# Out-projection of a decoder trunk: quarter sums by accumulating transfers, the residual seeded into PSUM, signs turned

## The chip, the core and the metric

The kernel runs on one core of a Trainium2 chip. TensorE (PE, with its weight loads shown as PEld) multiplies, VectorE (DVE) and ScalarE (ACT) do elementwise work, GpSimd (POOL) does a little arithmetic and issues transfers, SyncE (SP) issues most loads from HBM. Products land in PSUM, which here has eight banks of 128x512 float32; everything else on the core lives in SBUF. The metric is the time of one execution on the device in microseconds (us).

## The reference, cut to what matters

Two layers over 256 tokens of width 2048. In each layer the input is normalised and projected to q, k, v and three convolution parts; attention and a gated short convolution give two blocks of 1024 columns; one shared output projection adds them to the residual x; then comes a squared-ReLU MLP of width 8192.

```
for l in range(DEPTH):                                   # 2
    h = _rmsnorm(x, attn_norm_g[l])
    proj = h @ w_in[l]                                   # q k v gate_b gate_c conv_in
    ...
    x = x + jnp.concatenate([attn, conv], axis=-1) @ w_out[l]     # 2048 x 2048
    hm = _rmsnorm(x, mlp_norm_g[l]) @ w_up[l]
    x = x + jnp.square(jax.nn.relu(hm)) @ w_down[l]
```

All of it is float32.

## The kernel before

**Arithmetic.** Each float32 operand of a matmul is split into a rounded part `hi` (ScalarE, type float32r) and a remainder `lo` (VectorE, the value minus `hi`); a product is three matmuls, hi x hi, hi x lo, lo x hi (`TERMS`). A matmul takes a 128x128 block of activations as weights and streams 128x512 of the weight matrix.

**Seven products.** In part of the projections a block of two 128-row chunks of the contraction (a "pair", index i) times two 512-column chunks is not formed from eight products of quarters but from seven, with sums of quarters on both sides. The activation quarters are A11, A21, A12, A22 and the sums S1 to S4 (made by `BySeven.sums_of`); the weight quarters are two loads of 512 KB, `left` and `right`, and four sums `t`. The seven products gather in their own PSUM banks `prods[1..7]` over several pairs, and `results` joins them with a few adds. In the plan constants, an entry `("s", i)` is a seven-product pair and `(n, i)` an ordinary one for column chunk n.

**Stages.** Per layer: q and k side by side, v with attention behind it, the convolution parts, then the out-projection in a left half (columns 0 to 1023, interleaved with the gate's columns, plan `LEFT`) and a right half (columns 1024 to 2047, plan `RIGHT`), then the MLP. The right half's plan is

```
RIGHT = ((0, 0), (0, 1), (1, 0), (1, 1), (0, 4), (1, 4), ("s", 2), (0, 5), (1, 5), ("s", 3),
         (0, 6), (0, 7), (1, 6), (1, 7))
```

An ordinary pair is 12 matmuls and one load of 512 KB; a seven-product pair is 21 matmuls and two loads. While the right half runs, the first two chunks of the new x are already normalised and transposed for the MLP (`norm.chunk`, in the background), and the third and fourth follow as soon as the right half has finished them.

**Weights.** `Weights.take` makes the jobs of the next three entries ahead of the one that it returns. A plain job loads into one of four `raw` rooms and splits into `whi`/`wlo`, three rooms each (tags `hi`, `lo`). The jobs of a seven-product pair are `plain` (loads, the split `w7b` of B11 and B21, the split of B22 into `whi`/`wlo`), `sums` (on VectorE the four sums `w7t`, lines 916, 917, 921, 922, and the split `w7x` of the first two) and `more` (the split `w7y` of the last two). `w7b` and `w7t` lie in the pool of tag "b" with eight rooms, which also holds the four `cat` tiles (the activations of the out-projection, four 128-row chunks each) and the activation sums; `w7x` and `w7y` lie in the two "bias" rooms. In `seven` the products come in the order 1, 2, 3 (plain quarters), 5, 7 (`w7x`), 6, 4 (`w7y`).

**Order.** TensorE's order is the program's. On the other engines and the queues a planner sets the order once, when the kernel is built, from a model of the times and the program's order as priority; each engine and each queue then works in that order and waits for semaphores. Rooms of a pool are handed on by such waits.

**Ends.** In `results` the seven products become e1 to e4 (one ScalarE copy, lines 972 to 976), which `add` puts onto x (line 980) when the half is done; the two ordinary chunks are added to x by lines 1061 and 1167. The first matmul into a bank opens it (`start=True`) and so overwrites what was there. The MLP's down-projection uses the same seven products (`quarters`, lines 1330 to 1334; the activation sums in `square`, lines 1452 to 1455; `seven_onto`).

Of the kernel before, what the change touches and what calls it, by code (L numbers as in the profile page):

```python
# [15 lines left out]
P = 128  # L16
# [117 lines left out]
def trunk(ctx: ExitStack, tc: tile.TileContext, x, w_in, w_out, conv_w, q_norm_g, k_norm_g,  # L134
# [370 lines left out]

    class Norm:
# [10 lines left out]
        def chunk(self, n, wait):  # L517
# [5 lines left out]
            for j in range(2):  # L523
# [12 lines left out]
                else:  # L536
                    y = wide(f"ny{pair}").rearrange("p (k s) -> p k s", k=2)
                    for i in range(2):
# [5 lines left out]
                    self.sums_of(pair, *(y[:, i, t * P:(t + 1) * P]  # L544
                                         for i in range(2) for t in range(NT)))
# [288 lines left out]
    A11, A21, A12, A22, S1, S2, S3, S4 = range(8)  # L834

    class BySeven:
# [9 lines left out]
        def sums_of(self, i, a11, a21, a12, a22):  # L846
# [18 lines left out]
        def jobs(self, w, i, cols, in_keys=False):  # L865
# [44 lines left out]
            def sums():  # L910
                left, right = mine["raw"]
                pool, tag = (self.kpool, "kL") if in_keys else (self.pool, "b")
                t = mine["t"] = pool.tile([P, 4, CH], F32, tag=tag, name="w7t")

                with behind(in_keys or self.rooms_of == 8):
                    nc.vector.tensor_sub(t[:, 0], right[:, 0], left[:, 0])
# [5 lines left out]
                nc.vector.tensor_sub(t[:, 3], left[:, 1], t[:, 2])  # L922
                return made
# [4 lines left out]

            return [plain, sums, more]

        def form(self, i, pa, a):

            if a >= S1:
                return self.sums[i][pa][:, a - S1]
# [3 lines left out]
        def product(self, n, i, a, b, start, stop):  # L938

            for m, (pa, pw) in enumerate(TERMS):  # L940
                nc.tensor.matmul(self.prods[n], self.form(i, pa, a), b[pw],  # L941
                                 start=(start and m == 0), stop=(stop and m == 2))

        def pair(self, i, chunks, starts=(), last=False):

            for n, accs in chunks:
                hi, lo = self.weights.take()
                for j in range(2):
# [8 lines left out]
                    for t, pa, pw in steps:  # L957
# [3 lines left out]
                            stop=(last and j == 1 and (pa, pw) == TERMS[-1]))  # L961
                    work.tick()

        def results(self, n):
# [7 lines left out]
            nc.scalar.activation(e1, prods[1], AF.Copy)  # L972
            nc.vector.tensor_add(e2, prods[6], e1)
            nc.vector.tensor_add(e4, prods[5], e2)
            nc.vector.tensor_add(x22, prods[5], x22)
            nc.vector.tensor_add(e3, prods[7], e2)

            def add():
                for x_, e in ((x11, e1), (x21, e3), (x12, e4), (x22, e3)):
                    nc.vector.tensor_add(x_, x_, e)  # L980

            return add
# [15 lines left out]
        def left(self, acts, cv):  # L998
# [8 lines left out]
            def column(c):  # L1007
# [8 lines left out]
                if c % 2 and i in SEVEN_LEFT + SEVEN_RIGHT:  # L1016
                    self.sums_of(i, *(y[:, k, t * P:(t + 1) * P]
                                      for k in range(2) for t in range(NT)))

            def banks():  # L1020
# [3 lines left out]
                for n in (5, 7, 4):  # L1024
                    prods[n] = bank(f"po{l}{n}")

            for j, (what, i) in enumerate(LEFT):
# [4 lines left out]
                elif what == "a":  # L1032
# [5 lines left out]
                    self.product(2, i, A12, b21, start, not {"a", 0} & rest)  # L1038
                    self.product(3, i, S4, b22, start, not {"a", 1} & rest)
                    self.product(5, i, S1, self.t1, start, end)  # L1040
                    work.tick()
                elif what == "b":
# [5 lines left out]
                    if end:  # L1048
                        add = self.results(0)
                else:  # L1050
                    opening = what == 1 and 8 not in prods
                    if opening:
                        prods[8] = ps.tile([P, CH], F32, tag="av", name=f"po{l}8", bufs=1)
                    accs = ((prods[2], prods[4]), (prods[3], prods.get(8)))
# [698 lines left out]
```

## Time and profile before

| | |
|---|---|
| time, two runs | 2112.37 and 2113.86 us, median 2113.11 us |
| profiled execution, first to last instruction (its span) | 2110.7 us |
| median above that span | 2.4 us |
| granted TensorE clock, mean | 1.000 |
| HBM read | 440.52 MB |
| loads of w_out | 64 of 512 KB, 4.5 us from issue to landing |
| right half in layer 0 and in layer 1 | about 337 to 381 us and 1386 to 1430 us |

The profiled execution's own time is known only by its span; what lies around it is taken as the 2.4 us between span and median. A line of the profile's groups has source line, engine, operation, what it writes from what it reads, shape and count, then busy time, mean ns of one, and the idle time of the engine before it with what ended that. A line of the timeline has start and duration in us, engine, source line, operation and count. In the waits, a line gives who waited, for what, then the total in us, how often, and the longest.

### The profile page before, as it was taken

The page shows a single profiled execution, that of the slowest core. Times are in us where ns is not written, and L with a number is a line of the kernel's source. Part 1 is how long each engine was busy: PE and PEld are TensorE (multiplying, and loading weights), DVE is VectorE, ACT ScalarE, POOL GpSimd, SP SyncE. Part 2 cuts the span into 40 slices and gives each one's busy share as a digit, 9 for nine tenths or more (in the row PEclk, how much of TensorE's full clock was granted, in tenths as well). Part 3 has the DMA queues.
Part 4 walks back from the last instruction along what each step waited for, and adds up shares of the span by engine and source line. Part 5 has one row for each costly group of instructions (what it writes and reads, how often), then busy time and mean ns, then how long its engine had stood idle before and what let it go on. Part 6 is the DMA issues. An engine that isn't in the chain of part 4 may idle for free.

```text
span 2110.7 us, 29252 instructions
## 1 busy us (share of the span) xinstructions
PE 2105.2 (100%) x10809; PEld 1799.0 (85%) x10809; DVE 1834.6 (87%) x2525; ACT 1407.5 (67%) x1823; POOL 189.4 (9%) x226
## 2 busy tenths in 40 slices
PE   9999999999999999999999999999999999999999
PEld 7888888888888888888888888888888888888887
DVE  7888788898888888799888887988988888888998
ACT  6777566676776766666566775657676677675664
POOL 2211120000000000011101121000000000000110
PEclk9999999999999999999999999999999999999999
DMA  7655575887777777789566456668777777777993
GB/s 265 205 154 167 171 216 182 289 259 229 230 238 229 231 232 230 251 291 310 171 220 188 152 170 185 195 193 290 255 238 229 229 230 238 230 229 260 315 309 113
DMA packets 312607, 476.01 MB, mean 226 GB/s; under 512 B 12723, under 2 KB 209669, under 8 KB 312464
## 3 DMA queue, kind: packets, MB, share of 16 engines
q1 hardware_dynamic: 284752, 406.76, 60.7%
q0 software_dynamic: 27520, 67.24, 10.1%
q8 instruction: 85, 1.39, 0.3%
q14 instruction: 58, 0.48, 0.1%
q10 hardware_dynamic: 192, 0.15, 0.0%
HBM read 440.52 MB, written 33.58 MB: 225 GB/s over the span
## 4 chain that ended last, share of the span: by engine, by line
PE 98%; DMA 1%; POOL 1%; DVE 1%; issue 0%; ACT 0%; ACTq 0%; DVEq 0%
PE upc L1427 31%; PE pr L1470 14%; PE dn L1551 8%; PE gc L481 4%; PE ci L481 4%; PE gb L433 4%; PE v L456 3%; PE q L958 3%; PE o L958 3%; PE k L958 3%; PE dn L1470 3%; PE po L941 2%; PE dn L1645 2%; PE pr1r L1470 2%; PE pr0r L1470 2%; PE po L958 2%
## 5 line engine op out<-in xcount | busy, mean ns | idle before, releaser
L1427 PE MATMUL upc<-nT,uhi 128*128 128x512 f32 x1920 | 454.7, 389 | 0.0
L1427 PEld LDWEIGHTS upc<-nT,uhi 128*128 128x128 f32 x1920 | 360.2, 188 | 74.7
L1292 DVE TENSOR_TENSOR ulo<-uraw,uhi 128x1024 fp32r<-128x1024 f32 x256 | 312.3, 1222 | 109.8 <-ACT f L1459 91.5
L341 ACT ACTIVATE whi<-raw 128x1024 fp32r<-128x1024 f32 x232 | 244.7, 1058 | 180.2 <-issue 21.8
L1291 ACT ACTIVATE uhi<-uraw 128x1024 fp32r<-128x1024 f32 x256 | 270.6, 1057 | 135.7 <-PE upc L1427 115.4
L342 DVE TENSOR_TENSOR wlo<-raw,whi 128x1024 fp32r<-128x1024 f32 x232 | 284.3, 1234 | 53.1 <-ACT whi L341 46.9
L1427 PEld LDWEIGHTS upc<-nT,ulo 128*128 128x128 f32 x1920 | 246.2, 191 | 9.4
L1427 PE MATMUL upc<-nT,ulo 128*128 128x256 f32 x1920 | 249.1, 283 | 0.0
L1317 ACT ACTIVATE bh<-draw 128x1536 fp32r<-128x1536 f32 x86 | 128.3, 1492 | 103.7 <-PE pr L1470 82.1
L1318 DVE TENSOR_TENSOR bl<-draw,bh 128x1536 fp32r<-128x1536 f32 x86 | 151.3, 1759 | 11.4 <-ACT bh L1317 10.9
L1551 PE MATMUL dn<-whi,fb 128*128 128x512 f32 x480 | 152.0, 389 | 0.0
L1470 PE MATMUL pr<-bh,f 128*128 128x512 f32 x360 | 121.4, 391 | 0.0
L341 ACT ACTIVATE whi<-uraw 128x1024 fp32r<-128x1024 f32 x60 | 63.7, 1062 | 72.0 <-PE dn L1551 58.5
L1437 ACT ACTIVATE ev<-upc 128x512 f32<-128x512 f32 x120 | 72.0, 600 | 54.0 <-PE upc L1427 54.0
L1317 ACT ACTIVATE t24h<-t 128x1024 fp32r<-128x1024 f32 x86 | 91.4, 1063 | 23.7 <-PE pr L1470 15.9
L1551 PEld LDWEIGHTS dn<-whi,fb 128*128 128x128 f32 x480 | 90.1, 188 | 18.6
L1318 DVE TENSOR_TENSOR t24l<-t,t24h 128x1024 fp32r<-128x1024 f32 x86 | 104.9, 1220 | 0.2
L1330 DVE TENSOR_TENSOR t<-draw 128x1024 f32<-128x1024 f32 x86 | 105.0, 1221 | 0.1
L1318 DVE TENSOR_TENSOR t13l<-t,t13h 128x1024 fp32r<-128x1024 f32 x86 | 104.9, 1220 | 0.0
L1317 ACT ACTIVATE t13h<-t 128x1024 fp32r<-128x1024 f32 x86 | 91.5, 1063 | 8.1 <-DVE t L1330 2.9
L1470 PE MATMUL pr<-t13h,f 128*128 128x512 f32 x240 | 93.8, 391 | 0.0
L1551 PE MATMUL dn<-wlo,fb 128*128 128x512 f32 x240 | 93.4, 389 | 0.0
(528 smaller groups left out, 4383.9 us busy)
## 6 DMA issues: line engine op xcount, KB each, us to landing
uraw<-in_w_up_dram SPq DMA_DIRECT2D x128, 1024.0 KB, 6.3
raw<-in_w_in_dram SPq DMA_DIRECT2D x191, 512.0 KB, 4.2
draw<-in_w_down_dram SPq DMA_DIRECT2D x180, 512.0 KB, 5.3
raw<-in_w_out_dram SPq DMA_DIRECT2D x64, 512.0 KB, 4.5
uraw<-in_w_down_dram SPq DMA_DIRECT2D x60, 512.0 KB, 6.8
hid0p<-f POOLq DMA_DIRECT2D x17, 512.0 KB, 3.5
fb<-hid0p POOLq DMA_DIRECT2D x17, 512.0 KB, 8.0
hid1p<-f POOLq DMA_DIRECT2D x17, 512.0 KB, 3.5
```

Source lines behind the costliest of these rows:

```text
L341: pair = (nc.scalar.activation(hi, raw, AF.Copy), nc.vector.tensor_sub(lo, raw, hi.bitcast(F32)))
L342: nc.vector.tensor_sub(lo, raw, hi.bitcast(F32)))
L481: nc.tensor.matmul(acc[:, f, 0] if part else acc[:, f], wt[:, k % 4, fs], a.ap[:, 0, k % KG] if part else a.ap[:, :, k % KG], start=(part ...
L958: nc.tensor.matmul(accs[t], a.ap[:, pa, k % KG, t * P:(t + 1) * P], (hi, lo)[pw][:, j], start=(j == 0 and (pa, pw) == (0, 0) and (n, t) in ...
L1291: pair = (nc.scalar.activation(hi, src, AF.Copy), nc.vector.tensor_sub(lo, src, hi.bitcast(F32)))
L1292: nc.vector.tensor_sub(lo, src, hi.bitcast(F32)))
L1317: keep(nc.scalar.activation(hi, src, AF.Copy))
L1318: keep(nc.vector.tensor_sub(lo, src, hi.bitcast(F32)))
L1330: keep(nc.vector.tensor_sub(t[:, 0:2], raw[:, 0::2], raw[:, 1::-1]))
L1427: nc.tensor.matmul(acc[:, 0] if part else acc, wt[part][:, k], a.ap[:, 0, k % KG] if part else a.ap[:, :, k % KG], start=(part == 0 and kh ...
L1470: nc.tensor.matmul(prods[n], f[:, pa, a], b[pw], start=(start and m == 0), stop=(stop and m == 2))
L1551: nc.tensor.matmul(prods[p], f[:, pa, 2 * k + t], b[pw][:, n], start=(p in starts and k == 0 and m == 0), stop=(stop and k == 1 and m == 2))
```

## The change

1. **Quarter sums of the right half by transfers.** For the two seven-product pairs of the right half the jobs are new: `whole`, `summed`, `last`. Both loads go into one tile `w7r` of tag "b". After the plain quarters have been split, four transfers from POOL's queue add one quarter onto another in place (`accum_op=ALU.add`); what stands in the tile afterwards are the four sums, which are split into `w7x` and `w7y` as before. VectorE's four adds and `w7t` are gone there.
2. **Signs.** Since such a transfer can only add, the weight sums become pure additions everywhere (left half, q/k, MLP too), and the activation sums and the joining of products turn their signs to match. S3 and S1 now lie beside each other and are made by one operation where the quarters lie in one tile (`quarters_of`, `square`). In the q/k pairs all four weight sums are made ahead of the first split.
3. **Residual into the banks.** `seed` copies x into the ordinary banks by ScalarE (three banks of the left half, four of the right), and no matmul opens these. `results` then writes into x what it used to put into extra tiles, and the extra adds onto x are gone except one in the left half.

```diff
-    A11, A21, A12, A22, S1, S2, S3, S4 = range(8)
+    A11, A21, A12, A22, S3, S1, S2, S4 = range(8)
...
             v = wide(f"sv{i}").rearrange("p (s c) -> p s c", c=P)
-            nc.vector.tensor_add(v[:, 0], a21, a22)
-            nc.vector.tensor_sub(v[:, 1], v[:, 0], a11)
-            nc.vector.tensor_sub(v[:, 2], a11, a21)
-            nc.vector.tensor_sub(v[:, 3], a12, v[:, 1])
+            if both is None:
+                nc.vector.tensor_sub(v[:, 0], a11, a21)
+                nc.vector.tensor_sub(v[:, 1], a21, a22)
+            else:
+                nc.vector.tensor_sub(v[:, 0:2], *both)
+            nc.vector.tensor_sub(v[:, 2], v[:, 1], a11)
+            nc.vector.tensor_add(v[:, 3], a12, v[:, 2])
...
+                def rest():
+                    nc.vector.tensor_add(t[:, 2], t[:, 0], right[:, 1])
+                    nc.vector.tensor_add(t[:, 3], left[:, 1], t[:, 2])
+
                 with behind(in_keys or self.rooms_of == 8):
-                    nc.vector.tensor_sub(t[:, 0], right[:, 0], left[:, 0])
-                    nc.vector.tensor_sub(t[:, 1], right[:, 1], right[:, 0])
+                    nc.vector.tensor_add(t[:, 0], left[:, 0], right[:, 0])
+                    nc.vector.tensor_add(t[:, 1], right[:, 0], right[:, 1])
                 room = self.biasp.tile([P, 2, 2, CH], F32R, tag=self.spare, name="w7x")
+                if self.rooms_of == 8:
+                    rest()
                 made = two(room, t[:, 0:2])
-
-                nc.vector.tensor_add(t[:, 2], t[:, 1], left[:, 0])
-                nc.vector.tensor_sub(t[:, 3], left[:, 1], t[:, 2])
+                if self.rooms_of != 8:
+                    rest()
                 return made
...
+            def whole():
+
+                raw = mine["raw"] = self.pool.tile([P, 2, 2, CH], F32, tag="b", name="w7r")
+                for n in range(2):
+                    nc.sync.dma_start(
+                        raw[:, :, n], w[2 * P * i:2 * P * (i + 1),
+                                        cols[n]:cols[n] + CH].rearrange("(k p) c -> p k c", p=P))
+                room = self.pool.tile([P, 2, 2, CH], F32R, tag="b", name="w7b")
+                b11, b21 = two(room, raw[:, :, 0])
+                hi = wpool.tile([P, 2, CH], F32R, tag="hi", name="whi")
+                lo = wpool.tile([P, 2, CH], F32R, tag="lo", name="wlo")
+                b22 = split(hi[:, 0], lo[:, 0], raw[:, 1, 1])
+                for k, n, by in ((0, 0, (0, 1)), (0, 1, (1, 1)), (1, 1, (0, 0)), (1, 0, (1, 1))):
+                    nc.gpsimd.dma_start(raw[:, k, n], raw[:, by[0], by[1]], accum_op=ALU.add)
+                return b11, b21, b22
+
+            def summed():
+                room = self.biasp.tile([P, 2, 2, CH], F32R, tag=self.spare, name="w7x")
+                return two(room, mine["raw"][:, 0])
+
+            def last():
+                room = self.biasp.tile([P, 2, 2, CH], F32R, tag=self.spare, name="w7y")
+                return two(room, mine["raw"][:, 1])[::-1]
+
+            if by_transfer:
+                return [whole, summed, last]
             return [plain, sums, more]
...
+        def seed(self, *places):
+
+            for n, t, acc in places:
+                nc.scalar.activation(acc, xs[n][:, t], AF.Copy)
 
         def results(self, n):
...
-            room = self.tmp.tile([P, 2, CH], F32, tag="ao", name="es", bufs=1)
-            e1, e2, e3 = room[:, 0], wide("e2"), room[:, 1]
-            e4 = self.kpool.tile([P, CH], F32, tag="kL", name="es4")
-            nc.scalar.activation(e1, prods[1], AF.Copy)
-            nc.vector.tensor_add(e2, prods[6], e1)
-            nc.vector.tensor_add(e4, prods[5], e2)
-            nc.vector.tensor_add(x22, prods[5], x22)
+            e2, e3 = wide("e2"), x21 if n else wide("e3")
+            nc.scalar.activation(x11, prods[1], AF.Copy)
+            nc.vector.tensor_add(e2, prods[6], x11)
+            nc.vector.tensor_sub(x12, prods[5], e2)
             nc.vector.tensor_add(e3, prods[7], e2)
-
-            def add():
-                for x_, e in ((x11, e1), (x21, e3), (x12, e4), (x22, e3)):
-                    nc.vector.tensor_add(x_, x_, e)
-
-            return add
+            nc.vector.tensor_sub(x22, prods[5], e3)
+            if not n:
+                nc.vector.tensor_add(x21, x21, e3)
...
-                    self.weights.jobs += self.jobs(w, i, (2 * CH, 3 * CH))
+                    self.weights.jobs += self.jobs(w, i, (2 * CH, 3 * CH), by_transfer=True)
...
-            opened, add = set(), None
+            for n in range(2):
+                self.seed(*((2 + n, t, accs[n][t]) for t in range(NT)))
...
-                    keep(nc.vector.tensor_sub(t[:, 0:2], raw[:, 0::2], raw[:, 1::-1]))
+                    keep(nc.vector.tensor_add(t[:, 0:2], raw[:, 1:3],
+                                              raw[:, 0:1].to_broadcast([P, 2, CH])))
...
-                    nc.vector.tensor_add(h[:, S1], h[:, A21], h[:, A22])
+                    nc.vector.tensor_sub(h[:, S3:S1 + 1], h[:, A11:A21 + 1], h[:, A21:A22 + 1:2])
                     nc.vector.tensor_sub(h[:, S2], h[:, S1], h[:, A11])
-                    nc.vector.tensor_sub(h[:, S3], h[:, A11], h[:, A21])
-                    nc.vector.tensor_sub(h[:, S4], h[:, A12], h[:, S2])
+                    nc.vector.tensor_add(h[:, S4], h[:, A12], h[:, S2])
```

More of the change, by code (lines that the diff above doesn't have):

```diff
@@ L1048, in left @@
                     if end:
-                        add = self.results(0)
+                        self.results(0)
                 else:
@@ L1157, in right @@
                     if i == SEVEN_RIGHT[-1]:
[L1158 removed]
+                        self.results(2)
                     continue
[L1160 to L1164 removed]
+                self.pair(i, [(what, accs[what])], (), not {"s", what} & rest)
                 if not {"s", what} & rest:
```

56 lines of the change are left out of this document (26 added, 30 removed).

## The prediction

> **What bounds the kernel now.** I read the page's first part, then the waits of the weight loader, then the stage that the change touches by windows, and last its single instructions. The page:
>
> ```profile
> span 2110.7 us, 29252 instructions
> PE 2105.2 (100%) x10809; PEld 1799.0 (85%) x10809; DVE 1834.6 (87%) x2525; ACT 1407.5 (67%) x1823; POOL 189.4 (9%) x226
> ```
>
> TensorE lacks 5.5 us of the span (2110.7 - 2105.2). A busy PE can hide slow issue, so the waits of its loader come next, whole kernel, longest first, cut to those that touch the change:
>
> ```profile
> PEld po0r L941 <- DVE w7y L880: 0.5, 1, 0.5
> PEld po L941 <- DVE w7y L880: 0.2, 1, 0.2
> ```
>
> and the windows (columns: stretch, length, then busy time of PE, PEld, DVE, ACT, POOL, clock, DMA share, GB/s) of the out-projection's right half in layer 0, its middle, and the steady part of the MLP:
>
> ```profile
> 340.00:394.00 54.00, 54.00 (x271) 45.33 (x270) 45.44 (x66) 33.05 (x51) 0.89 (x2) 1.00 0.74 242
> 345.00:369.00 24.00, 24.00 (x111) 19.88 (x110) 22.12 (x30) 15.78 (x21) 0.00 (x0) 1.00 0.59 184
> 420.00:900.00 480.00, 480.00 (x2551) 415.46 (x2550) 422.47 (x542) 329.68 (x360) 21.05 (x34) 1.00 0.76 235
> ```
>
> PE is never idle there and the clock is full. The chain of waits shows that it also issues at its full pace: 12 matmuls of an ordinary pair take 24 / 48 of this, 2.72 us for each pair, 0.227 us for a matmul.
>
> ```profile
> 369.93 10.89 PE o L958 x48
> ```
>
> The diff changes no matmul's shape or count. So nothing that it takes off VectorE or ScalarE can shorten the kernel by more than the 5.5 us, and of these only the 0.7 us of the two waits above is near it. The question is whether something new makes TensorE wait.
>
> **The change, part by part.**
>
> *Work that leaves VectorE.* Groups by line (busy us, mean ns):
>
> ```profile
> L1452 DVE TENSOR_TENSOR h<-h 128x128 f32<-128x128 f32 x60 | 17.1, 284 | 0.0
> L980 DVE TENSOR_TENSOR x<-x,es 128x512 f32<-128x512 f32 x16 | 10.4, 685 | 0.0
> L916 DVE TENSOR_TENSOR w7t<-raw 128x512 f32<-128x512 f32 x2 | 1.4, 688 | 1.0 <-DMA raw<-in_w_out_dram 1.0
> ```
>
> In the MLP two 128x128 operations become one of twice the width, at most 17.1 us off VectorE. `results` goes from 8 operations on VectorE to 5 in each left half and to 4 in each right half, 7 x 2 x 0.685 = 9.6 us less. The four sums of each of two pairs per layer go, 4 x 4 x 0.688 = 11.0 us. All of it runs under a TensorE that is 100% busy in its windows: worth 0. The turned signs exchange one operation for another of the same size: 0. In the q/k pairs the other two sums (0.69 us each) now stand ahead of the first split. Layer 0's second half is the nearest:
>
> ```profile
> 91.85 1.22 DVE L880 TENSOR_TENSOR w7x<-w7t,w7x 128x1024 fp32r<-128x1024 f32 x1
> 92.99 0.69 DVE L922 TENSOR_TENSOR w7t<-raw,w7t 128x512 f32<-128x512 f32 x1
> 94.72 1.52 PE L941 MATMUL po0r<-w7x,sf 128*128 128x512 f32 x6
> ```
>
> One of them is there already; the other pushes the end of the split from 93.07 to 93.76, still 1.0 us ahead of its first matmul. Without that cover it would cost at most 0.7 us, in five places.
>
> *Seeds.* Seven 128x512 copies a layer from x into PSUM, on ScalarE, ahead of matmuls that no longer open their bank. The nearest row is the eviction of one bank; the tightest place is the right half's second pair of banks, which VectorE's last adds of the left half (third row) release:
>
> ```profile
> 366.22 0.58 ACT L972 ACTIVATE es<-po0r 128x512 f32<-128x512 f32 x1
> 337.76 0.61 ACT L559 ACTIVATE junk<-x 128x512 f32<-128x512 f32 x1
> 336.31 1.88 DVE L1061 TENSOR_TENSOR x<-po,x 128x512 f32<-128x512 f32 x3
> 342.39 0.48 PE L958 MATMUL o<-whi,cat 128*128 128x512 f32 x1
> ```
>
> The bank is released at 338.2 (336.31 + 1.88) or before; two copies make 339.4, and behind four squares of 0.61 that start at 337.76 they end at 341.4. The second chunk's first matmul is at 342.39 (last row): 0, and if ScalarE's order is worse, two copies, 1.2 us a layer.
>
> *The transfers.* This is the new dependency. A seven-product pair needs plain quarters first, then the sums w7x, then w7y. Now the sums come from four transfers of 128x512 f32 (256 KB) issued from POOL, each adding one quarter onto another of the same tile. They are a chain: 2 writes what 1 reads, 3 reads what 1 writes and writes what 2 reads, 4 reads what 3 writes. Transfer 1 overwrites a quarter that ScalarE and VectorE must have split (w7b); transfer 3 overwrites the one that is split into whi/wlo. w7x waits for 2, w7y for 4. Here is where these stand now, on ScalarE, VectorE, TensorE:
>
> ```profile
> 343.50 1.06 ACT L879 ACTIVATE w7b<-raw 128x1024 fp32r<-128x1024 f32 x1
> 348.80 0.62 ACT L879 ACTIVATE whi<-raw 128x512 fp32r<-128x512 f32 x1
> 351.38 0.69 DVE L880 TENSOR_TENSOR wlo<-raw,whi 128x512 fp32r<-128x512 f32 x1
> 355.28 1.22 DVE L880 TENSOR_TENSOR w7y<-w7t,w7y 128x1024 fp32r<-128x1024 f32 x1
> 356.11 1.06 ACT L879 ACTIVATE w7b<-raw 128x1024 fp32r<-128x1024 f32 x1
> 358.21 0.84 PE L941 MATMUL po0r<-w7y,sf 128*128 128x512 f32 x3
> 368.41 0.84 PE L941 MATMUL po0r<-w7y,sf 128*128 128x512 f32 x3
> ```
>
> Four dependent 0.69 us adds that had 1.7 us to spare (355.28 + 1.22 = 356.50 against 358.21) become four dependent transfers. No row shows an accumulating transfer, or one inside the chip. The nearest are POOL's own stores from SBUF, twice the bytes, in the MLP where the DMA share is 0.76; under them the shortest store and the other form of store:
>
> ```profile
> DMA to landing us min/median/max: 3.1/3.5/9.7
> hid0p<-f POOLq DMA_DIRECT2D x17, 512.0 KB, 3.5
> by_dist_d<-setup POOLq DMA_DIRECT2D x1, 23.9 KB, 2.4
> hid0s<-h POOLq DMA_DIRECT2D x13, 512.0 KB, 6.4
> ```
>
> So one transfer, t, costs from 2.4 (almost no bytes) to 9.7 us. I take 3.5: half the bytes of hid0p, but two reads for one write, so about the same traffic. The Trainium skill, "DMA: Bandwidth & Descriptors", section on the anatomy of one DMA from gpsimd, fits a transfer as 2.0 us plus its bytes over 436 GB/s; that estimate would be 2.6 us here, and then, by the formulas below, TensorE would wait for nothing. The 3.5 and 6.4 us rows of this trace lie above that formula's 3.2 us for 512 KB.
>
> First pair. Its two loads wait now for "raw" rooms, on SP, and the w7b split on VectorE follows them:
>
> ```profile
> 339.35 0.37 SPq L895 DMA_DIRECT2D raw<-in_w_out_dram  x1
> 342.54 0.37 SPq L895 DMA_DIRECT2D raw<-in_w_out_dram  x1
> 344.59 1.23 DVE L880 TENSOR_TENSOR w7b<-raw,w7b 128x1024 fp32r<-128x1024 f32 x1
> ```
>
> With the change both go into one "b" room, of which three are free once the left half is done (eight, less four of cat and one of sums); so they can be issued before 339.35, nothing behind them on SP is held up, and transfers 1 and 2 can be over by 351. The third waits for wlo of the fourth quarter. Its whi room comes free with TensorE's pair (1,1), so it stays near 348.80; its VectorE half ends at 352.07 now and near 350.3 with the w7t and w7x operations ahead of it gone. I take 351. w7y is ready at 351 + 2t + 2.3 (1.06 + 1.22), wanted at 358.21: wait 2t - 4.9, which is 2.1 us for 3.5. Were the loads no earlier than now, transfer 1 would start at 345.8 and the wait be 345.8 + 4t + 2.3 - 358.21 = 4t - 10.1, 3.9 us.
>
> Second pair. Its w7b room is free once cat's first tile is done with (pair (1,1), about 348.6), and its data is loaded early; I put the w7b split's end at 355. POOL is one queue: transfer 1 of this pair stands behind transfer 4 of the pair before, and can go when that one is issued, 351 + t. Ready at max(355, 351 + t) + 4t + 2.3, wanted at 368.41. For 3.5: 371.3, a wait of 2.9 us. The chain runs by its own clock, so the first wait is contained in this: 2.9 us a layer. What else queues behind POOL's waits: nothing in 345 to 369 (POOL busy 0.00). Behind w7y on ScalarE and VectorE stand the splits for the pair that follows; TensorE needs those only after w7y.
>
> *Sum.* 2 x 2.9 = 5.8, less 0.2 of the `po` wait, 5.6 us: span 2116.3. The median of the two runs, 2113.11, is 2.4 above the span of the profiled execution; with the same 2.4 I get 2118.7, so 2119.
>
> **The rivals.**
> - *The transfers stay hidden.* With t at 2.8 or below the second pair's wait, 355 + 4t + 2.3 - 368.41, is 0 and the first's 0.7 at most. For it: the 2.4 us row, and a start ahead of 355 would add to it. Against: 3.1 is the shortest store of the hid0p line. Time: 2112 to 2114. The fit of the Trainium skill's DMA page falls into this case.
> - *Transfers of 5 to 7.2 us*, as hid0s takes with 4 KB rows. Then the wait is 351 + 5t + 2.3 - 368.41 = 5t - 15.1 a layer: 9.9 for 5, 16.9 for 6.4. Time 2133 at 5, 2147 at 6.4.
> - *The chain becomes the stage's bound, and the kernel is slower by more than 2%.* 42.3 us are 21.1 a layer: 5t - 15.1 = 21.1 at t = 7.25. At the worst row, 9.7 us: 33.4 a layer, 2180. For it: the accumulate is unseen, the uraw stream of the MLP starts at 369.96 and fills the engines. Against: the median rows all lie below 7.25, and the DMA share is 0.59 in these 24 us.
> - *Waits go away.* If all of the 5.5 us that TensorE is not busy went, the time would be 2107.6. A gain of 42 us is not there to be had.
> - *A seed that doesn't count* (a first matmul that overwrites the bank) would lose the residual and cost no time.
>
> The row behind the two places:
>
> ```profile
> 369.96 0.99 SPq L1284 DMA_DIRECT2D uraw<-in_w_up_dram  x2
> ```
>
> **How the numbers follow.** About 2% (42 us) is what a measurement of this kernel can tell from no change. Chances: forecast, t from 2.8 to 5, 2114 to 2133: 0.45. Hidden: 0.33. Five to 7.25: 0.13. Beyond: 0.07. Some waits gone: 0.02. The range 2112 to 2141 leaves out transfers above some 5.7 us (5t - 15.1 = 13.4, twice that is 27), about 0.17, and the gain, 0.02. Within 2% lie all of these but "beyond"; 0.01 is kept for a gain that no row here offers: faster 0.01, same 0.92, slower 0.07.
>
> **What would show it.** In the changed profile: a DMA group raw to raw on POOL's queue, 4 x 2 x 2 = 16 transfers, with its median t; a wait of PEld at `product` for w7y, in the second pair near 368 us, of about 3 us a layer, absent if the transfers are hidden; TensorE's other windows unchanged at 100%; no wait at the seeds. I am wrong if TensorE waits at w7x or at a seed, if waits show up in the MLP, or if t lies outside 2.4 to 5.

## The result, and the profile after

The kernel after takes 2135.99 us (median of two runs, 2134.27 and 2137.72) against 2113.11 before: a ratio of 1.011, 95% interval 1.0094 to 1.0127. It is slower by 22.9 us, within 2%. The forecast was 2119; its sign and its range (2112 to 2141) held, but the size is four times the 5.6 us that it had worked out, and most of it comes from waits that were not in the sum, as counted below. The page of the changed kernel, its first lines:

```profile
span 2132.5 us, 29207 instructions
PE 2115.0 (99%) x10809; PEld 1803.6 (85%) x10809; DVE 1814.2 (85%) x2430; ACT 1413.2 (66%) x1837; POOL 188.9 (9%) x242
```

VectorE has lost 20.4 us of work (1834.6 to 1814.2), of the 37.7 at most that the prediction's three terms add up to, and the kernel gained nothing from it. The span is 21.8 us longer (2110.7 to 2132.5). TensorE now lacks 17.5 us of its span, where it lacked 5.5. The waits of the weight loader, the longest first (who waited, for what, total in us, times, longest):

```profile
PEld o L997 <- ACT whi L341: 4.9, 2, 2.5
PEld po0r L979 <- DVE w7y L887: 4.2, 4, 1.9
PEld po1r L979 <- ACT w7y L886: 3.1, 1, 3.1
PEld o L997 <- DVE wlo L342: 2.1, 2, 1.1
PEld po0r L979 <- ACT w7y L886: 1.3, 2, 1.0
PEld po1r L979 <- DVE w7y L887: 1.1, 1, 1.1
```

Two kinds stand there. The waits for `w7y` were forecast, if not their size; the longest in the second row, 1.9 us, is another one, found below. The first and the fourth row were not: these are ordinary matmuls of the right half (`o`, line 997), which wait for the split of an ordinary weight load. Their place is the second entry of the plan, (0, 1). TensorE there, in layer 0:

```profile
340.26 0.39 PE L997 MATMUL o<-whi,cat 128*128 128x512 f32 x1
342.55 0.66 PE L997 MATMUL o<-whi,cat 128*128 128x512 f32 x1 [1.90 <-ACT whi L341]
343.81 0.80 PE L997 MATMUL o<-wlo,cat 128*128 128x512 f32 x1 [0.60 <-DVE wlo L342]
344.41 1.05 PE L997 MATMUL o<-whi,cat 128*128 128x512 f32 x2
345.26 0.63 PE L997 MATMUL o<-wlo,cat 128*128 128x512 f32 x1
```

One matmul stands between a gap of 2.29 us (340.26 to 342.55) and one of 1.26 us. Then a third thing begins: two matmuls fill 344.41 to 345.26, 0.427 us each instead of 0.227, and ten of them do. The windows show it as a granted clock of 0.66, where the same stretch had 1.00 before:

```profile
340.00:350.00 10.00, 7.50 (x21) 5.32 (x20) 4.73 (x4) 8.47 (x16) 0.00 (x0) 0.66 0.67 219
```

So a wait costs more than its length: after the longer ones TensorE runs at half pace for another 3.5 to 5.4 us in this kernel.

Why was the ordinary load late? SyncE's queue of the changed kernel, then ScalarE:

```profile
312.20 0.46 SPq L945 DMA_DIRECT2D w7r<-in_w_out_dram  x1
315.15 0.37 SPq L383 DMA_DIRECT2D raw<-in_w_out_dram  x1
315.56 0.46 SPq L945 DMA_DIRECT2D w7r<-in_w_out_dram  x1
319.33 0.97 SPq L383 DMA_DIRECT2D raw<-in_w_out_dram  x2
323.68 0.88 SPq L945 DMA_DIRECT2D w7r<-in_w_out_dram  x2
324.66 0.48 SPq L383 DMA_DIRECT2D raw<-in_w_out_dram  x1
325.25 3.57 SPq L1316 DMA_DIRECT2D uraw<-in_w_up_dram  x2
328.91 15.24 SPq L383 DMA_DIRECT2D raw<-in_w_out_dram  x5
```

```profile
332.53 1.06 ACT L341 ACTIVATE whi<-raw 128x1024 fp32r<-128x1024 f32 x1 [1.66 <-PE po L997]
341.44 1.06 ACT L341 ACTIVATE whi<-raw 128x1024 fp32r<-128x1024 f32 x1 [7.86 <-DMA raw<-in_w_out_dram]
```

Ahead of the raw loads that the right half needs first, there now stand all four w7r loads (2 MB) and two loads of the MLP's w_up (1 MB each); before, the first w_up load was issued at 369.96. ScalarE sits idle for 7.86 us until the raw load lands. It is the load issued at 328.91, the first of the queue's last row; from issue to landing it took

```profile
DMA to landing us min/median/max: 12.5/12.5/12.5
```

where the loads of w_out before had a median of 4.5. In the stretch 332 to 342 the load on the DMA engines, before and after, is

```profile
332.00:342.00 10.00, 10.00 (x45) 8.23 (x45) 7.31 (x9) 5.94 (x12) 0.00 (x0) 1.00 0.63 199
```

```profile
332.00:342.00 10.00, 8.65 (x39) 6.82 (x37) 3.93 (x6) 1.62 (x2) 0.00 (x0) 1.00 1.08 366
```

a share of 0.63 at 199 GB/s before, of 1.08 at 366 GB/s after. The transfers themselves, with their median from issue to landing, and their shortest, median and longest:

```profile
w7r<-w7r POOLq DMA_DIRECT2D x16, 256.0 KB, 4.5
DMA to landing us min/median/max: 3.2/4.5/8.4
```

Counting by how much each matmul starts later than 0.227 us after the one ahead of it (right halves, both layers): gaps at the second entry 3.5 and 3.7 us; gaps at w7y 2.8 in layer 0 (1.8 in the first pair, 1.0 in the second) and 3.9 in layer 1 (first pair alone); 28 matmuls at half pace, 28 x 0.20 = 5.6 us. That is 19.5 of the 21.8 us. Of what is left, 1.4 us is in a place that has nothing to do with the right half: the q and k projections of layer 0, found below.

### The profile page after: what moved, and what is told of

Read it like the earlier page. It is cut to its first block, busy times and chain, and to the rows that moved or that the text cites. A ratio compares the mean times of both kernels' runs of the same rounds, so it can differ in the third digit from the quotient of the medians.

```text
span 2132.5 us, 29207 instructions
## 1 busy us (share of the span) xinstructions
PE 2115.0 (99%) x10809; PEld 1803.6 (85%) x10809; DVE 1814.2 (85%) x2430; ACT 1413.2 (66%) x1837; POOL 188.9 (9%) x242
## 4 chain that ended last, share of the span: by engine, by line
PE 79%; issue 2%; DMA 1%; DVE 0%; ACT 0%; POOL 0%; POOLq 0%; ACTq 0%
PE upc L1460 31%; PE pr L1502 14%; PE dn L1585 8%; PE dn L1502 2%; PE gc L481 2%; PE ci L481 2%; PE v L456 2%; PE gb L433 2%; PE dn L1679 2%; PE q L997 2%; PE k L997 2%; PE pr1r L1502 2%; PE pr0r L1502 2%; PE o L997 1%; DMA w7r<-w7r 1%
```

## The experiments

All ratios are to the kernel before on the same chip, with 95% intervals; it took 2112.4 to 2112.7 us there. "Held" below means that `results` takes its two extra tiles again.

### Two tiles held, the transfers kept

Theory: `results` no longer takes the tile "ao" and a tile of "kL", so the MLP's rooms that lie over them come free early, the w_up loads move ahead of raw loads, and that is the wait at the second entry.

```diff
-            e2, e3 = wide("e2"), x21 if n else wide("e3")
+            room = self.tmp.tile([P, 2, CH], F32, tag="ao", name="es", bufs=1)
+            e2, e3 = room[:, 0], self.kpool.tile([P, CH], F32, tag="kL", name="es4")
```

> The changed kernel with one part undone: the joining of the products again takes its two extra tiles, so that the rooms in which the MLP's first w_up loads will lie come free as late as before; transfers, seeds and signs stay. Theory A (two early w_up loads stand ahead of the out-projection's loads on SP and starve the right half's second pair; about 6 us a layer with the slow clock behind it): no wait at whi/wlo near 340 us, the waits at w7y stay, 2122 to 2127 us. Theory B (the early loads of the transfers' own tiles, 2 MB a layer, do the starving): the wait near 340 stays, 2134 to 2138 us.

Measured 2125.84 us, ratio 1.0062 (1.0047 to 1.0077), in theory A's range. The first w_up load goes out at 374.86 and the wait for a raw load is gone: 10 us of the 22.9. The rest stays at w7y, and a wait at a seed has appeared, which the changed kernel did not have:

```profile
PEld po0r L979 <- DVE w7y L887: 3.7, 3, 1.9
PEld po1r L979 <- ACT w7y L886: 3.6, 1, 3.6
PEld o L997 <- ACT o L1007: 3.0, 2, 1.9
```

### The early freeing kept, no transfers

```diff
-                    self.weights.jobs += self.jobs(w, i, (2 * CH, 3 * CH), by_transfer=True)
+                    self.weights.jobs += self.jobs(w, i, (2 * CH, 3 * CH), by_transfer=False)
```

> The changed kernel without the transfers: the right half's sums are made on VectorE again, with the turned signs; the early freeing of rooms and the seeds stay. Theory A: the w7y waits of 1.9 and 1.2 us in layer 0 and 5.6 us in layer 1 go, the two early w_up loads and part of their wait stay, 2115 to 2127 us. Theory C (the transfers alone cost the 22.9 us, through their traffic or their waits): 2112 to 2115 us, with no wait near 340.

Measured 2113.76 us, ratio 1.0006 (0.9996 to 1.0015). Two w_up loads still go out at 325.34 and 328.01, and TensorE waits for nothing in the right half. Early w_up loads alone do no harm: in this form theory A is wrong, and the time is the one of theory C. But C, the transfers alone, doesn't fit the run above, where 10 us went with w_up's place while the transfers stayed. So w_up's loads do harm beside the w7r loads or the transfers.

### Two tiles held and no transfers: only signs, seeds and shorter joining

Both edits above.

> Both of these undone: what is left of the change is the signs, the seeds and the shorter joining. Both theories: the time of before, 2111 to 2115 us; TensorE waits at no seed. If the seeds or the signs cost something, it shows here above 2115 us.

Measured 2113.52 us, ratio 1.0004 (0.9995 to 1.0013). VectorE has 10.8 us less to do (1823.8 against 1834.6), which is worth nothing, and the seeds cost nothing. Its profiled span is 2112.3, 1.6 above before, and one wait is new, also in the changed kernel (its row among the waits of the weight loader, then VectorE's and TensorE's instructions):

```profile
PEld po0r L979 <- DVE w7y L887: 2.1, 2, 1.9
```

```profile
42.62 1.22 DVE L887 TENSOR_TENSOR w7y<-w7t,w7y 128x1024 fp32r<-128x1024 f32 x1
43.89 0.74 PE L979 MATMUL po0r<-w7y,sf 128*128 128x512 f32 x2 [1.51 <-DVE w7y L887]
```

It lies in the first q/k pair of layer 0. There VectorE's half of the w7y split ended at 42.4 before and ends at 43.8 now; TensorE's wait, 0.5 us before, is 1.9. The sums are not what moved it: in this pair all four stood ahead of the first split before, too. It comes from ScalarE's order. A split of an ordinary weight (`whi`, line 341), started at 29.99 before, stands behind four squares of the norm now and starts at 31.72; VectorE waits 1.79 us for it, where it waited 0.35, and stays about that late up to the w7y split.

### Two tiles held, transfers of half the size

Only the first 256 of 512 columns of each sum are made; the other half of the four sums is left out of the computation.

```diff
-                    nc.gpsimd.dma_start(raw[:, k, n], raw[:, by[0], by[1]], accum_op=ALU.add)
+                    nc.gpsimd.dma_start(raw[:, k, n, :CH // 2], raw[:, by[0], by[1], :CH // 2],
+                                        accum_op=ALU.add)
```

> The first kernel of this call with transfers of half the width (128x256 instead of 128x512), so half of each sum is left out. If a transfer's time is mostly fixed: 3.5 to 4.3 us against about 4.5 us and nearly the same waits at w7y. If it goes by bytes: about 2.3 to 3 us, and the waits at w7y shrink by 2 us a layer or more.

Measured 2123.88 us (three runs, 2119.68 to 2128.07), ratio 1.0053 (1.0037 to 1.0069). In the profiled execution (span 2117.9) the row of the transfers is

```profile
w7r<-w7r POOLq DMA_DIRECT2D x16, 128.0 KB, 3.0
```

3.0 us against 4.6 in the run with full transfers: 1.6 us go with 128 KB, and 1.4 us are left for nothing, if the two sizes lie on a line. With transfers half as long the gaps at w7y are 0.8 us at most in this execution; what TensorE waits for otherwise in the right halves is seeds, 2.3 us, and ordinary `wlo` splits, 1.9 us. The runs scatter by 8 us, so how much of the time the length is worth isn't settled by this one. The scatter goes with the clock: 2119.68 us came with a mean granted clock of 1.000, 2123.88 with 0.998 and 2128.07 with 0.996. A clock short by 0.002 over 2122 us is worth up to 4.2 us, by 0.004 up to 8.5 (an estimate from these figures), so half pace can account for it; where it lay no trace shows.

### The second pair's w7r loads late, w_up early

From the changed kernel: two copies of 128x1, which read a later weight's `hi`, stand ahead of the second pair's loads, so that the planner puts these at about the place of the kernel before.

```diff
                 raw = mine["raw"] = self.pool.tile([P, 2, 2, CH], F32, tag="b", name="w7r")
+                if i == SEVEN_RIGHT[-1]:
+                    seen = self.weights.made[-10][0]
+                    for n in range(2):
+                        nc.vector.tensor_copy(raw[:, 0, n, 0:1], seen[:, 0, 0:1].bitcast(F32))
```

> From the changed kernel, with `results` still freeing its two tiles early, so that the two w_up loads of 1 MB stay ahead of the raw loads; only the two w7r loads of the second seven-product pair (1 MB) are put back to about the place that the kernel before gives them (two 128x1 copies that read a late tile stand ahead of them). Theory of the queue (the raw loads are late because w_up's 2 MB and w7r's second megabyte stand ahead of them together; w_up's alone did no harm in the run without transfers): the wait at the second entry of the right half, 2.29 + 1.26 us and the half pace after it, goes, some 10 us in two layers: 2123 to 2128 us. Rival (the transfers' own traffic beside w_up's loads is enough): 2133 to 2137, with that wait as it was.

Measured 2128.76 us, ratio 1.0079 (1.0062 to 1.0096): between the two forecasts. ScalarE says why:

```profile
338.13 1.06 ACT L886 ACTIVATE w7x<-w7r 128x1024 fp32r<-128x1024 f32 x1 [4.21 <-DMA w7r<-w7r]
339.09 1.04 ACT L341 ACTIVATE whi<-raw 128x1024 fp32r<-128x1024 f32 x1
340.90 1.06 ACT L341 ACTIVATE whi<-raw 128x1024 fp32r<-128x1024 f32 x1 [0.76 <-DMA raw<-in_w_out_dram]
```

The raw load now costs it 0.76 us instead of 7.86. But in this kernel's order the split of w7x stands ahead of the ordinary splits, and it waits 4.21 us for transfer 2; behind them stand the seeds, for which TensorE waits 4.4 us in two places. One cause has taken the other's place.

### Two tiles held, the split of w7x late

```diff
                 room = self.biasp.tile([P, 2, 2, CH], F32R, tag=self.spare, name="w7x")
-                return two(room, mine["raw"][:, 0])
+                with behind(True):
+                    return two(room, mine["raw"][:, 0])
```

> From the run with two tiles held (2125.8 us), with one thing changed: the split of w7x of the first seven-product pair stands late in the order of ScalarE and VectorE, as the other splits of whole() do not, so that the splits of ordinary weights and the seeds no longer stand behind its wait for transfer 2. Theory (in-order engines behind a transfer): the waits at the seed of the second entry, 1.07 us in layer 0 and 1.97 in layer 1, go, and the w7y waits stay: 2121 to 2124 us. Rival (the seeds are late because VectorE's last adds of the left half are late for another reason): 2125 to 2127, seed waits as they were.

Measured 2123.22 us, ratio 1.005 (1.0035 to 1.0065), 2.6 us below the run with two tiles held. The two seed waits of that run, gaps of 1.07 and 1.97 us, less 0.23 each, are 2.6. They are gone; what is left is w7y in the first pair (and the q/k pair's 1.9 in the second row):

```profile
PEld po1r L980 <- ACT w7y L886: 3.8, 1, 3.8
PEld po0r L980 <- DVE w7y L887: 3.4, 3, 1.9
PEld po0r L980 <- ACT w7y L886: 1.1, 1, 1.1
```

### Two tiles held, the second pair's loads late

> From the run with two tiles held (2125.8 us), with the second pair's w7r loads put back to about the place of the kernel before. If the load that stands ahead of the raw loads also delays the left half's end and the seeds: 2120 to 2124 us, seed waits gone or halved. If only what stands behind transfers 2 to 4 counts: 2125 to 2127. If the later load makes the second pair's chain of transfers later: 2127 to 2131, with a longer wait at w7y of the second pair.

Measured 2133.19 us, ratio 1.0099 (1.0084 to 1.0114): slower than any of the three forecasts. The planner's order changed again, and w7x came to stand ahead of the seeds:

```profile
333.99 1.06 ACT L886 ACTIVATE w7x<-w7r 128x1024 fp32r<-128x1024 f32 x1 [6.72 <-DMA w7r<-w7r]
334.96 0.58 ACT L1011 ACTIVATE o<-x 128x512 f32<-128x512 f32 x1
335.48 1.04 ACT L341 ACTIVATE whi<-raw 128x1024 fp32r<-128x1024 f32 x1
```

ScalarE stands for 6.72 us behind a transfer whose result TensorE needs almost thirty microseconds later, while a seed and a split wait that TensorE needs now. TensorE waits for that split in the left half, in both layers, 7.6 us (four waits for whi and wlo of lines 341 and 342). The Trainium skill, "TensorE: Matmul & The Clock Gate", section on the array's architecture, says that ScalarE's and VectorE's queues are strictly first in, first out; these rows agree.

### Three cures together

Two tiles held, w7x late, the second pair's loads late, and the fourth quarter of each pair split into a room of its own, so that transfer 3 need not wait until TensorE gives a `whi` room back.

```diff
-                hi = wpool.tile([P, 2, CH], F32R, tag="hi", name="whi")
-                lo = wpool.tile([P, 2, CH], F32R, tag="lo", name="wlo")
-                b22 = split(hi[:, 0], lo[:, 0], raw[:, 1, 1])
+                if i == SEVEN_RIGHT[0]:
+                    hi, lo = (self.tmp.tile([P, CH], F32R, tag="s", name="w7q", bufs=2)
+                              for _ in range(2))
+                else:
+                    own = self.kpool.tile([P, 2, CH], F32R, tag="kL", name="w7q")
+                    hi, lo = own[:, 0], own[:, 1]
+                b22 = split(hi, lo, raw[:, 1, 1])
```

> From the run with two tiles held: w7x late as in one run, the second pair's loads late as in the other, and the fourth quarter of each of the two pairs split into a room of its own rather than into the whi and wlo rooms, so that transfer 3 no longer waits for a room that TensorE's ordinary pairs must give back. Theory (what remains is places in queues and a shared room, not the length of the transfers): w7y is ready ahead of TensorE in the first pair; in the second, whose first transfer can start when its w7b is split, about 350, 350 + 4 x 4.5 + 2.3 against about 368.4 leaves up to 1.9 us a layer: 2113 to 2117 us. Rival (the length of the four transfers and their traffic itself): waits of 2 us and more in both pairs, 2118 to 2124. In neither case faster than the kernel before, since TensorE is busy throughout.

Measured 2122.21 us (2117.03 to 2123.63), ratio 1.004 (1.0027 to 1.0053). The profiled execution is the one of 2117.03. In it the first pair waits for nothing, and in the second a gap of 0.8 us and one of 1.26 are left in each layer, 1.6 us beyond TensorE's pace, where up to 1.9 was forecast. POOL's and ScalarE's rows of that chain in layer 1:

```profile
1405.28 0.85 POOL L962 DMA_DIRECT2D w7r<-w7r  x1 [14.42 <-DVE w7b L887]
1409.18 0.86 POOL L962 DMA_DIRECT2D w7r<-w7r  x1 [3.05 <-DMA w7r<-w7r]
1412.98 0.86 POOL L962 DMA_DIRECT2D w7r<-w7r  x1 [2.95 <-DMA w7r<-w7r]
1416.42 0.86 POOL L962 DMA_DIRECT2D w7r<-w7r  x1 [2.59 <-DMA w7r<-w7r]
```

```profile
1419.72 1.06 ACT L886 ACTIVATE w7y<-w7r 128x1024 fp32r<-128x1024 f32 x1 [4.30 <-DMA w7r<-w7r]
```

Four transfers take 14.4 us, 3.6 each, and start only when the w7b split is done. The median lies in the rival's range, 2118 to 2124, but the rival's waits in both pairs are not in this trace. The other executions are up to 6.6 us longer than the profiled one. The two shortest, 2117.03 and 2118.82 us, had a granted clock of 1.000, the three longer ones, 2122.21 to 2123.63, of 0.998, which is worth up to some 4 us; so in those TensorE ran at half pace for a while. No trace here shows where; that the second pair's gaps grow past the point where the clock halves would fit, and is not shown.

### w_up early, the other causes eased

The changed kernel with the second pair's loads late and w7x late.

> From the changed kernel, its two tiles still freed early, so w_up's 2 MB stay ahead of the raw loads; the second pair's w7r loads late and the split of w7x late. Theory (two causes took each other's place: raw loads behind 3 MB in the changed kernel, ScalarE behind w7x's transfer once w7r was put late; with both gone the second entry of the right half doesn't wait): as in the run with tiles held and w7x late, only the first pair's w7y waits: 2121 to 2125 us. Rival (w_up's early loads delay the raw loads or the transfers by themselves): a wait at the second entry of 1 us and more remains, or w7y's is longer: 2126 to 2131.

Measured 2129.51 us, ratio 1.0079 (1.0064 to 1.0094): the rival. It differs from the run with w7x late in w_up's 2 MB, which are early, and in the second pair's loads, which are later, and is 6.3 us slower. ScalarE waits for raw loads again, 3.77 and 1.64 us (at 337.44 and 340.15), VectorE's last adds of the left half stand behind those splits, the seeds behind the adds, and TensorE has a gap of 2.04 us in layer 0 and of 2.31 in layer 1.

### w_up and w7r early, w7x late, the fourth quarter in its own room

> From the changed kernel, its loads left as they are, w_up's and the second pair's w7r's both ahead of the raw loads; w7x late and the fourth quarter in a room of its own, so that nothing waits for transfer 2 on ScalarE too soon and nothing for transfer 3's room. What is left is the late raw loads and the second pair's chain. Theory: the wait at the second entry stays, 2.3 + 1.3 us and half pace, some 5 us a layer, and about 2 us a layer at the second pair's w7y as in the run with all three cures: 2121 to 2128 us. Rival (the raw loads were late only through something that these two edits remove): 2115 to 2119.

Measured 2136.17 us, ratio 1.0111 (1.0096 to 1.0126): neither forecast. w_up's loads moved to 358.48, apparently since the new rooms for the fourth quarter lie where the MLP's do, and the wait at the second entry is gone. But now they fall into the second pair's chain:

```profile
354.49 0.87 POOL L958 DMA_DIRECT2D w7r<-w7r  x1 [11.42 <-DVE w7b L887]
358.46 0.87 POOL L958 DMA_DIRECT2D w7r<-w7r  x1 [3.10 <-DMA w7r<-w7r]
366.57 0.87 POOL L958 DMA_DIRECT2D w7r<-w7r  x1 [7.24 <-DMA w7r<-w7r]
370.05 0.87 POOL L958 DMA_DIRECT2D w7r<-w7r  x1 [2.61 <-DMA w7r<-w7r]
```

```profile
358.48 10.62 SPq L1321 DMA_DIRECT2D uraw<-in_w_up_dram  x2
```

The transfer issued at 358.46, together with the w_up loads, holds up the next one until 366.57, 8.1 us; the one before it took 4.0 and the one after it 3.5. TensorE waits 8.4 us at w7y in layer 0 and 6.4 in layer 1 (and 1.1 at w7x there). Layer 1 shows the same: the transfer issued at 1418.56, beside w_up's loads of 1418.10, holds up the next one for 8.6 us, the ones around it took 4.5 and 4.0. That a transfer's time depends on what loads run beside it is shown here.

### Transfers in the first pair only

Two tiles held, w7x late, the fourth quarter in its own room; the second pair keeps its sums on VectorE.

```diff
-                    self.weights.jobs += self.jobs(w, i, (2 * CH, 3 * CH), by_transfer=True)
+                    self.weights.jobs += self.jobs(w, i, (2 * CH, 3 * CH),
+                                                   by_transfer=i == SEVEN_RIGHT[0])
```

> Two tiles held, w7x late, the fourth quarter in its own room, and transfers only in the first seven-product pair; the second keeps its sums on VectorE. Theory (of the run with all three cures what remained was the second pair's chain, four transfers of about 3.6 us from the end of its w7b split, about 405 in layer 1's count to w7y; the first pair's chain is hidden): no wait of TensorE at w7x or w7y: 2112 to 2114.5 us. Rival (transfers cost something beside the wait, by the DMA share or the rooms): 2115 to 2119. Not below 2111 by either, since TensorE is busy throughout.

Measured 2113.7 us, ratio 1.0005 (0.9996 to 1.0015), with no wait in either right half. Eight accumulating transfers are hidden completely when nothing stands behind them.

### The same early loads, the sums by VectorE in the same places

```diff
-                for k, n, by in ((0, 0, (0, 1)), (0, 1, (1, 1)), (1, 1, (0, 0)), (1, 0, (1, 1))):
-                    nc.gpsimd.dma_start(raw[:, k, n], raw[:, by[0], by[1]], accum_op=ALU.add)
...
+            def add(*places):
+                raw = mine["raw"]
+                for k, n, by in places:
+                    nc.vector.tensor_add(raw[:, k, n], raw[:, k, n], raw[:, by[0], by[1]])
...
+                with behind(True):
+                    add((0, 0, (0, 1)), (0, 1, (1, 1)))
...
+                add((1, 1, (0, 0)), (1, 0, (1, 1)))
```

> From the changed kernel: the same early loads (w_up's 2 MB and all four w7r loads ahead of the raw loads), the same rooms and seeds, but the four sums of a pair are made in the same places by VectorE instead of by transfers, so that no transfer inside the chip is left. If the early loads alone make the raw loads late: the wait at the second entry of the right half stays at about 2.3 + 1.3 us with half pace after it, some 5 us a layer, and the w7y waits go: 2120 to 2125 us. If the transfers' own traffic is needed to make them late: no wait there, 2112 to 2116. VectorE has 4 x 4 x 0.69 us more to do than in the changed kernel, as in the kernel before, beside a TensorE that is busy.

Measured 2119.53 us, ratio 1.0031 (1.002 to 1.0043): between the two. ScalarE waits for the raw load in both layers, less long than the 7.86 and 7.20 us of the changed kernel:

```profile
338.75 1.06 ACT L341 ACTIVATE whi<-raw 128x1024 fp32r<-128x1024 f32 x1 [4.82 <-DMA raw<-in_w_out_dram]
1390.26 1.06 ACT L341 ACTIVATE whi<-raw 128x1024 fp32r<-128x1024 f32 x1 [4.93 <-DMA raw<-in_w_out_dram]
```

What reaches TensorE at the second entry is one gap of 1.1 us in each layer, at full clock, instead of 2.3 to 2.5 and 1.26 and half pace. A gap of 1.24 us a layer at w7y comes from VectorE's adds just ahead of that split. So the early loads alone make the raw load late: issued at 327.70 it took 11.0 us to land. With the transfers it was issued 1.2 us later and took 1.5 us longer (328.91, 12.5 us), so the split starts 2.7 us later. Those 2.7 us and the changed order around them make a long gap of a short one; how much of it is the transfers' traffic alone isn't separated.

## Why the prediction was right or wrong, step by step

- *TensorE is the bound, VectorE's savings are worth 0.* Right: with only these left the ratio is 1.0004.
- *The q/k sums ahead of the first split: 0, at worst 0.7 us.* The wait grew by 1.4 us, and not through the sums. I took layer 0's second half as the tightest place; the first pair was tighter, and its wait of 0.5 us already stood in the rows that I had quoted. There the changed operations gave ScalarE another order, with a split behind four squares. That the planner could reorder a stage whose work hardly changes was not among the terms.
- *Seeds: 0.* Right without transfers. Beside them, seeds and ordinary splits stood behind w7x in ScalarE's order in several runs; I had looked only at what stands behind w7y.
- *t at 3.5 us.* The median is 4.5, within the bounds; 3.6 where little else runs (second pair of the run with three cures), 8.1 beside w_up's loads. This term was mis-sized because t was taken as one number.
- *First pair, 2t - 4.9.* The mechanism held. Where TensorE isn't held up earlier (w7x late, layer 0) transfer 3 is issued at 351.60, forecast 351, and the gaps there make 1.8 us, forecast 2.1 (2.7 with the 7.6 us that the two transfers took). In layer 1 the two transfers took 10.3 us instead of 7.6, which the formula turns into a longer wait: 4.5 us measured there, 5.4 by the formula (10.3 - 4.9).
- *Second pair, 2.9 us, containing the first.* Wrong: POOL's order put its transfer 1 (second row) ahead of transfer 4 of the first pair (third row), and in the changed kernel it waits 1.0 us in layer 0 and not at all in layer 1. By accident 1.8 + 1.0 comes near the 2.9 us a layer that were forecast; in layer 1 it is 3.9 and half pace.

```profile
357.34 0.88 POOL L954 DMA_DIRECT2D w7r<-w7r  x1 [26.48 <-DVE wlo L887]
358.82 0.87 POOL L954 DMA_DIRECT2D w7r<-w7r  x1 [0.61 <-DVE w7b L887]
360.85 0.87 POOL L954 DMA_DIRECT2D w7r<-w7r  x1 [1.15 <-DMA w7r<-w7r]
```

- *"So they can be issued before 339.35, nothing behind them on SP is held up."* This is the step that failed most. I moved four loads of 512 KB ahead and looked for instructions that wait in the queue, not for bytes that stand in front of other bytes: the load behind them took 12.5 us instead of some 4.5. And I overlooked what the shorter `results` frees: w_up's loads came too, since the tiles it gave up lie under the MLP's rooms. Holding the two tiles takes 10 us away; early w_up alone costs nothing; early loads without transfers show a gap of 1.1 us a layer at that entry; all three together make 3.5 us a layer and half pace.
- *No half pace.* It wasn't in the sum at all: 28 matmuls, 5.6 us, as much as the whole forecast. With the 7.2 us at the second entry and the 1.4 us in the q and k projections, 14 of the 21.8 us have causes that the forecast didn't have. That the time still lies in its range is luck.
- *The rivals.* The measured time lies in the interval of "transfers of 5 to 7.2 us" (2133 to 2155) for another reason: the median was 4.5. "Hidden" is what the first pair shows as soon as nothing stands in its way.
- *The signs.* The sixteen transfers, their median within 2.4 to 5 and the seeds that nobody waits for came as named. TensorE's other windows did not stay as they were: the wait at the second entry, in ordinary matmuls, was in none of the signs.
- *Two slips in the working.* At 2.6 us for a transfer the formula for the first pair gives 2 x 2.6 - 4.9 = 0.3 us a layer, not nothing. And 12 matmuls are 12 of the 48 in the row, not 24; the 2.72 us is right. Neither changes the forecast.

What stays open: where the runs with three cures and with half transfers, which scatter by 7 and 8 us, run at half pace, how much the transfers' traffic adds to the late load, and whether there is an order in which both pairs are hidden. No run was faster than the kernel before, and by the first step none can be by more than a few microseconds.

## What to carry to other kernels

Before moving a load earlier, add up the bytes that will then stand ahead of every load that is needed sooner; and when a tile is given up, look up which loads were waiting for its room. An engine that works in order must not reach an instruction that waits for a transfer before it has done what the bound engine needs sooner: late in the order was worth 2.6 us here, early cost up to 7. Moving work off an engine that isn't the bound pays nothing, and a chain of transfers in its place is a new way to be late.

## What the runs showed of the hardware that was not expected

- *The clock halves after a short wait.* After gaps between TensorE's starts of 2.29 + 1.26 us (changed kernel, layer 0), 2.50 + 1.26, 3.05 + 1.26 and 3.73 + 1.26 us, matmuls take 0.427 us instead of 0.227 for 2 to 5 us. After 1.0 + 1.26, 1.97 and 2.04 us they don't. Single gaps between go both ways: 2.28 us without (w7r late, layer 0), 2.21 with (the same run, layer 1). The Trainium skill, "TensorE: Matmul & The Clock Gate", part 1, has half rate after an idle window of about 3.4 us that runs freely, and 426.7 ns for a matmul of 512 columns at that rate. The pace agrees to the nanosecond, but a gap of 2.2 us was enough here, so a gap of 3.4 us is no safe limit. The traces' records of the granted clock show what decides. In all fourteen of them the clock changes only at whole steps of 3.413 us from the trace's first record, and a halved clock lasts one, two or three steps. Adding up the time within each step in which TensorE had no matmul (one of 512 columns taken as 0.23 us), it was at least 2.06 us in the step before each of the fourteen halvings ahead of a kernel's end, and at most 1.95 us in any step at full clock that no halving followed. The 2.28 us that went without fell into two such steps, the 2.21 us into one.
- *An accumulating transfer inside the chip* of 256 KB takes 4.5 us at the median of 16 (3.2 to 8.4), one of 128 KB 3.0.
